# A two-layer streaming encoder: values of the memory as split products, keys 256 columns wide, and low parts of 35 chunks kept in DRAM

## Chip, cores and metric

The kernel runs on one core of one Trainium2 chip. The metric is the device time of one execution in microseconds; three executions of the kernel before took 1884.56, 1885.33 and 1886.70 us, a median of 1885.33. The execution that the profiler recorded took 1886.81 us.

## What is computed

One inference step of a small encoder of two layers, for 384 tokens of width 1024: 256 frames of a new stream (the prompt) and 8 running streams of 16 frames (the sample). Each layer is an FFN, a token mixer (a convolution module in layer 0, a gated DeltaNet in layer 1), cross-attention into 256 memory tokens, and a second FFN, each with a norm ahead of it and behind it.

```python
def trunk(x, mem_k, mem_v, conv_bufs, dn_states, dn_bufs, P):
    for i in range(DEPTH):
        x = x + 0.5 * post(swiglu(pre(x)))              # f00, f10
        x = x + post(conv(pre(x)) or deltanet(pre(x)))  # conv, dn
        x = x + post(memory_cross_attention(pre(x), mem_k[i], mem_v[i]))   # x0, x1
        x = x + 0.5 * post(swiglu(pre(x)))              # f01, f11

def conformer_conv_module(h, conv_buf, ...):
    val, gate = jnp.split(h @ w_in + b_in, 2, axis=-1)
    u = val * jax.nn.sigmoid(gate)
    c = causal_depthwise_conv(concat([conv_buf, u]), dw) + dw_b     # 31 taps
    return jax.nn.silu(layer_norm(c)) @ w_out + b_out

p_mem_k = jnp.einsum('bmd,lde->lbme', mem_prompt, xa_wk)
p_mem_v = jnp.einsum('bmd,lde->lbme', mem_prompt, xa_wv)
```

(The loop over the layers is shortened here; `post` and `pre` are RMS norms with gains.) The last two lines are what the change touches most: the keys and values of the memory, for both layers, are 256 x 1024 times 1024 x 1024 each. They don't depend on the tokens, are outputs of the kernel, and are read by the cross-attention of their layer. Everything is float32.

## The kernel before

**Two kinds of matmul.** Most products are made from split operands. A weight chunk (128 x 1024 numbers, 512 KB) is loaded into one of three `raw` buffers; ScalarE casts it to a rounded high part `whi` (type float32r) and VectorE subtracts, which gives the low part `wlo` (`Emitter.get`, with `act` at L189 and `tt` at L197). Both parts lie in one of eight slots (W = 8), which are handed out in turn; `done` gives a slot back. Activations are split in the same way (`hTh` and `hTl`, `rbh` and `rbl`). A product is then three matmuls: high x high, high x low, low x high. The other kind multiplies float32 as it is: each such matmul appears in the profile as two MATMUL records. The keys and values of the memory are of this kind.

**Memory jobs.** There are 32 of them (`kvq`): for each layer and each of four heads two for keys and two for values, each one chunk of 128 output columns. A job (`kv`) takes 16 matmuls of 128 columns, ScalarE copies the 128 x 256 result out, and a store on GpSimd's queue brings it to the output `out_pkv`. The memory itself (two chunks) and four chunk slots lie in a region of their own (`kv_open`). The table `KV` says how many jobs are put at which stage as filling: 3 at the start, 3 at the end of the first FFN, 20 in the convolution, 3 behind it, and 1 and 2 in the two FFNs that follow.

**Stages.** `ffn` goes through 22 slices f of the hidden width: a gate chunk and an up chunk (24 matmuls of 384 columns each), then a down chunk of an earlier slice (18 matmuls of 512 columns). The first FFN, f00, runs from about 24 to 297 us; from f = 10 on it also spawns `old_taps`, which computes those taps of the convolution that need only the cache. `conv` makes 8 pairs of gate and value chunks (`cg`, `cv`), each pair closed by `glu`; `taps` then goes through the 31 taps of two channel groups at a time on VectorE (`stt`, L210). After the last tap come the layer norm by token tiles (`ln`) and the output projection with 8 `co` chunks and the bias row `bout` (`tokenwise`), which prepares the next norm (`chain`).

**Order.** The program is written down as operations with costs, and `Scheduler.order` puts them in order for each engine by a list schedule: among the operations that are ready, the one goes first whose remaining path plus `bonus` is longest. The order on each engine is then fixed; an instruction that waits holds up those behind it on its engine. Loads (`load`, L283) are issued by SyncE's queue, stores (`store`, L286) by GpSimd's, which also computes the powers of the norms (L197, L204).

Of the kernel before, what the change touches and what calls it, by code (L numbers as in the profile page):

```python
# [8 lines left out]
F32 = mybir.dt.float32  # L9
F32R = mybir.dt.float32r  # L10
AF = mybir.ActivationFunctionType
ALU = mybir.AluOpType
# [3 lines left out]
P = 128  # L16
D = 1024
KT = 8
# [6 lines left out]
XH = 4  # L25
MEM = 256
# [6 lines left out]
START = ["c0a", "m0a", "c0b", "m0b", "m1", "i", "x1", "g", "c1", "x2", "x0", "c2"]  # L33
TOLD = CW - BL
OLD = 10
CHB = 4000.0
RUSH = 10000.0
NRUSH = 3
SLOTS = 4
FOUR = ["f01", "f10", "f11", "x0", "x1"]  # L40

SPLIT = {"f00": 0, "conv": 0, "x0": 1, "f01": 0, "f10": 0, "dn": 1, "x1": 2, "f11": 0}

KV = {"start": 3, "f00": 3, "conv": 20, "co": 3, "xo": 0, "f01": 1, "f10": 2, "dn": 6, "f11": 0}
HALF = 1400.0
# [22 lines left out]
def chunk_names():  # L68
    names = [("mem", 0), ("mem", 1), ("bout",)]
    for l in range(2):  # L70
        for i in range(2):
            for f in range(FF):
                names += [("g", l, i, f), ("u", l, i, f), ("d", l, i, f)]
            names += [(n, l, i, j) for n in ("g4", "u4") for j in range(4)]
        names += [("q4", l, 0, j) for j in range(4)]
        for k in range(KT):
            names += [("wq", l, k), ("wo", l, k), ("wk", l, k // 2, k % 2), ("wv", l, k // 2, k % 2)]
    for k in range(KT):
        names += [("cg", k), ("cv", k), ("co", k)]
    names.append(("ab",))  # L80
    for h in range(NH):
        names += [("q", h), ("k", h), ("v", h), ("z", h), ("do", h)]
    return names


CHUNK = {n: i for i, n in enumerate(chunk_names())}


# [5 lines left out]
class Emitter:  # L94
# [3 lines left out]
    def __init__(self, nc):  # L98
        self.nc = nc
        self.q = []  # L100
        self.vt = 0.0
        self.ck = {"A": 0.0, "V": 0.0, "G": 0.0}
        self.tasks = []
        self.nchunk = 0
        self.names = []
        self.dest = {}
        self.bonus = 0.0
# [181 lines left out]
    def get(self, name, dest=None):  # L289
# [9 lines left out]
        self.act(hi, raw)  # L299
        self.tt(lo, raw, hi.bitcast(F32), ALU.subtract)  # L300
        return j, hi, lo

    def done(self, j):
# [13 lines left out]
class Scheduler:  # L317
# [10 lines left out]
    def cell(self, ap):  # L328
# [6 lines left out]
        if r is not None:  # L335
            return r
        if name.startswith(("in_", "out_")):
            r = (name, ap.offset // (P * D)) if name == "out_pkv" else (None, 0)
# [155 lines left out]
class Model:  # L494
    def __init__(self, nc, tc, A, O, s, ps):
        self.nc, self.A, self.O = nc, A, O
        E = self.E = Emitter(nc)
        E.wall = A["w"]
        E.held = [None] * W
        E.tc = tc  # L500
# [20 lines left out]
        self.hready = [0.0] * TT  # L521
        self.kvq = [(k, l, h, i) for l in range(2) for h in range(XH) for k in ("wk", "wv") for i in range(2)]
        self.kvroom, self.kvs, self.kvn = None, {}, 0
# [230 lines left out]
    def ffn(self, l, i, chains, post, pre):  # L754
# [68 lines left out]
        for f in range(first, FF):  # L823
# [10 lines left out]
            up(f, *p, bg, ou, bu, eu)  # L834
            E.bonus = 0.0
            for _ in range(2):
                if ndown < min(f, FF - TAIL):
                    down(ndown)
                    ndown += 1
# [38 lines left out]
    def kv_open(self, slots=2, order=()):  # L878
# [13 lines left out]
        return True  # L892

    def early(self, what, order):

        self.E.bonus = 1e9 - 1e6 * order.index(what) if what in order else 0.0
# [19 lines left out]
    def kv(self, n):  # L916
# [11 lines left out]
        for _ in range(n):  # L928
# [6 lines left out]
            o, b = self.bank()  # L935
            for m in range(2):
                c = slice(m * P, (m + 1) * P)
                for k in range(KT):
                    a, b_ = (w[:, k, :], mem[:, k, c]) if kind == "wk" else (mem[:, k, c], w[:, k, :])
                    E.mm(o[:, c], a, b_, k == 0, k == KT - 1)  # L940
            E.act(res, o[:, 0:MEM], dep=0)
            self.bfree(b)
            dst = self.O["pkv"][l, h]
            if kind == "wk":
                E.store(dst[:, i * MEM:(i + 1) * MEM], res)
            else:
                E.store(dst[:, 512:1024].rearrange("p (m d) -> p m d", m=2)[:, :, i * P:(i + 1) * P],
                        res.rearrange("p (m d) -> p m d", m=2))
            if len(self.kvq) >= self.kvslots:
# [28 lines left out]
    def conv(self, chains, post, pre):  # L978
# [62 lines left out]
        prefetch(1)  # L1041
        for c in range(KT):
            if c == 0:
                (og, bg, eg), (ov, bv, ev) = self.first_chunks([("cg", c), ("cv", c)], chains, SPLIT["conv"])
            else:
                og, bg, eg = self.proj(("cg", c))
                ov, bv, ev = self.proj(("cv", c))
            glu(c, og, bg, eg, ov, bv, ev)
            if c + 2 < KT:
                prefetch(c + 2)  # L1050

        self.kv(KV["conv"])
        E.wait(tapper)
# [655 lines left out]
def pack(inp):  # L1709
# [14 lines left out]
    for n, i in CHUNK.items():  # L1724
# [3 lines left out]
        elif t == "bout":  # L1728
            w[i, 0] = f("ca_b_out")[0]
        elif t in ("g4", "u4", "q4"):  # L1730

            a = wq[n[1]] if t == "q4" else (wg if t == "g4" else wu)[n[1], n[2]]
            w[i] = a[n[3] * 256:n[3] * 256 + 256, 0:512].reshape(2, P, 512).transpose(1, 0, 2).reshape(P, D)
# [4 lines left out]
        elif t == "wq":  # L1738
            w[i] = g_type(wq[n[1]], n[2] * P)
        elif t in ("wk", "wv"):  # L1740
            w[i] = g_type((wk if t == "wk" else wv)[n[1]], n[2] * MEM + n[3] * P)
        elif t == "wo":
# [77 lines left out]
```

## Time and profile before

| | |
|---|---|
| time, median of three | 1885.33 us |
| profiled execution | 1886.81 us |
| its span, first to last instruction | 1885.0 us |
| TensorE (PE), busy | 1860.1 us, 99% |
| VectorE (DVE) | 1011.6 us, 54% |
| ScalarE (ACT) | 753.8 us, 40% |
| GpSimd (POOL) | 170.2 us, 9% |
| read from HBM, written | 265.09 MB, 11.92 MB |
| granted clock of TensorE | 0.999 |

Matmuls are pipelined, so a matmul's own duration in the profile is longer than the time after which the next one starts; where the cost of many matmuls is meant, the distance between starts is the number to use. The chain that ended last is the profile's account of what set the end: it goes back from the last instruction to what released it. A row of a window gives the busy time of each engine in a stretch of the span, the clock, the share of time that the DMA engines were busy and the rate in GB/s. "Idle before" and "<-" name what an engine waited for. The time "to landing" of a load runs from its issue to its arrival.

### The profile page before, as it was taken

Reading aid. Unit: us, or ns where it says so; the run is one execution under the profiler, and the core shown is the slowest. Engines: PE = TensorE matmul, PEld = TensorE weight load, DVE = VectorE, ACT = ScalarE, POOL = GpSimd, SP = SyncE. Lnnn points to the kernel's source line nnn. Section 1 sums busy time; section 2 is a strip of 40 time slices with the busy share of each in tenths; the row PEclk is TensorE's granted clock in tenths of the full one; section 3 lists DMA queues with packets and bytes.
Section 4 is the critical chain, followed back from the end, with each engine's and each line's share of the span. In section 5 each row is a group of like instructions: output and inputs, shape, how many; then the busy total and the mean of one; then the engine's idle time right before and its main releaser. Section 6 shows DMA issues by size and latency. Waiting matters only on the chain.

```text
span 1885.0 us, 27534 instructions
## 1 busy us (share of the span) xinstructions
PE 1860.1 (99%) x10895; PEld 1682.0 (89%) x10895; DVE 1011.6 (54%) x1708; ACT 753.8 (40%) x1435; POOL 170.2 (9%) x391
## 2 busy tenths in 40 slices
PE   8999999999999999999999999999999999999998
PEld 8999999999877899999899999999998766899997
DVE  6564436999553633333633333688776734533333
ACT  4333334312643632333433233676564534432332
POOL 1000002111100100000100000323221101000000
PEclk9999999999999999999999999999999999999999
DMA  8543434556686534434434333323325682444331
GB/s 303 178 136 126 134 112 122 127 147 219 213 314 216 157 123 134 132 125 130 154 115 131 123 124 111 118 79 116 126 93 165 228 316 74 137 132 135 123 123 45
DMA packets 88466, 278.81 MB, mean 148 GB/s; under 512 B 18001, under 2 KB 20561, under 8 KB 88337
## 3 DMA queue, kind: packets, MB, share of 16 engines
q1 hardware_dynamic: 86080, 271.42, 44.8%
q0 software_dynamic: 2256, 5.64, 0.9%
q8 instruction: 85, 1.39, 0.3%
q14 instruction: 45, 0.36, 0.1%
HBM read 265.09 MB, written 11.92 MB: 147 GB/s over the span
## 4 chain that ended last, share of the span: by engine, by line
PE 94%; DVE 1%; DMA 1%; ACT 1%; POOL 1%; issue 1%; SPq 0%; DVEq 0%; POOLq 0%; ACTq 0%
PE ps L247 89%; PE ps L279 3%; PE ps L259 2%; POOL stat L197 1%; DVE big L210 1%; ACT big L190 1%; DMA big<-in_cv 0%; DMA x<-in_x 0%; DMA raw<-in_w 0%; PE ps L272 0%; DVE big L197 0%; ACT hTl L190 0%; ACT whi L189 0%; DMA big<-in_state 0%; DVE wlo L197 0%
## 5 line engine op out<-in xcount | busy, mean ns | idle before, releaser
L197 DVE TENSOR_TENSOR wlo<-raw,whi 128x1024 fp32r<-128x1024 f32 x361 | 438.6, 1222 | 581.4 <-ACT whi L189 555.7
L189 ACT CAST whi<-raw 128x1024 fp32r<-128x1024 f32 x361 | 374.5, 1051 | 652.5 <-PE ps L247 603.5
L247 PE MATMUL ps<-hTh,wlo 128*128 128x384 f32 x1680 | 495.4, 339 | 0.0
L247 PE MATMUL ps<-hTh,whi 128*128 128x384 f32 (+1 forms) x1680 | 494.5, 340 | 0.1
L247 PE MATMUL ps<-hTl,whi 128*128 128x384 f32 x1680 | 493.8, 340 | 0.0
L247 PEld LDWEIGHTS ps<-hTh,whi 128*128 128x128 f32 x1680 | 308.7, 188 | 8.0 <-ACT big L190 1.0
L247 PEld LDWEIGHTS ps<-hTl,whi 128*128 128x128 f32 x1680 | 308.8, 188 | 6.9 <-issue 1.5
L247 PEld LDWEIGHTS ps<-hTh,wlo 128*128 128x128 f32 x1680 | 309.0, 188 | 4.2 <-issue 0.4
L247 PE MATMUL ps<-big 128*128 128x128 f32 (+3 forms) x1912 | 283.7, 286 | 9.9 <-DMA big<-in_w 6.4
L247 PEld LDWEIGHTS ps<-big 128*128 128x128 f32 x1912 | 256.7, 193 | 35.0 <-issue 17.8
L247 PE MATMUL ps<-whi,rbh 128*128 128x512 f32 x672 | 205.2, 396 | 0.4 <-DVE big L210 0.4
L247 PE MATMUL ps<-wlo,rbh 128*128 128x512 f32 x672 | 203.0, 395 | 0.0
L247 PE MATMUL ps<-whi,rbl 128*128 128x512 f32 x672 | 201.7, 394 | 0.0
L210 DVE SCALAR_TENSOR_TENSOR big<-big,cols 128x384 f32<-128x384 f32 (+13 forms) x424 | 189.3, 499 | 2.6 <-ACT big L190 0.3
L247 PEld LDWEIGHTS ps<-whi,rbl 128*128 128x128 f32 x672 | 125.7, 188 | 24.8 <-issue 0.4
L247 PEld LDWEIGHTS ps<-wlo,rbh 128*128 128x128 f32 x672 | 125.3, 188 | 24.6 <-issue 0.8
L247 PEld LDWEIGHTS ps<-whi,rbh 128*128 128x128 f32 x672 | 124.9, 188 | 20.5 <-DVE big L210 0.6
L279 PE MATMUL ps<-ident,big 128*128 128x128 f32 x479 | 86.0, 275 | 6.0 <-DVE big L210 5.6
L247 PE MATMUL ps<-whi,hTh 128*128 128x512 f32 x240 | 87.7, 401 | 0.2 <-ACT hTh L189 0.2
L197 DVE TENSOR_TENSOR big<-big,ps 128x384 f32<-128x384 f32 (+4 forms) x131 | 67.2, 519 | 36.2 <-PE ps L247 36.1
L247 PE MATMUL ps<-whi,hTl 128*128 128x512 f32 x240 | 86.4, 398 | 0.1
L204 POOL TENSOR_SCALAR stat<-stat 128x1 f32<-128x1 f32 (+2 forms) x48 | 16.8, 350 | 767.6 <-ACT hTl L190 754.0
(84 smaller groups left out, 1337.8 us busy)
## 6 DMA issues: line engine op xcount, KB each, us to landing
raw<-in_w SPq DMA_DIRECT2D x362, 512.0 KB, 3.7
big<-in_w SPq DMA_DIRECT2D x37, 512.0 KB, 4.7
big<-in_ck SPq DMA_DIRECT2D x32, 512.0 KB, 6.3
big<-in_cv SPq DMA_DIRECT2D x32, 512.0 KB, 6.6
big<-in_npre SPq DMA_DIRECT2D x8, 512.0 KB, 7.5
big<-in_npost SPq DMA_DIRECT2D x8, 512.0 KB, 6.2
out_pkv<-big POOLq DMA_DIRECT2D x32, 128.0 KB, 5.1
big<-out_pkv SPq DMA_DIRECT2D x8, 512.0 KB, 6.3
```

The costliest lines, as they stand in the source:

```text
L189: return self._on("A", cost, dep, lambda: sc.copy(out, in_), [in_], w)
L190: return self._on("A", cost, dep, lambda: sc.activation(out, in_, func, **kw), [in_, bias, scale] + ([] if after is None else [after]), w, ...
L197: return self._on(eng, cost, dep, lambda: e.tensor_tensor(out=out, in0=a, in1=b, op=op), [a, b], [out])
L204: return self._on(eng, cost, dep, lambda: e.tensor_scalar(out=out, in0=a, scalar1=s1, scalar2=s2, op0=op0, **kw), [a, s1, s2 if s2 is not ...
L210: lambda: v.scalar_tensor_tensor(out=out, in0=a, scalar=s, in1=b, op0=op0, op1=op1), [a, s, b], [out])
L247: self._add("P", cost, lambda: t.matmul(out, lhsT, rhs, start=start, stop=stop, **kw), [lhsT, rhs], [out])
L259: t.matmul(out, lhsT, rhs, start=start, stop=stop)
L279: self._add("P", 109.0, lambda: t.transpose(out, in_, ident), [in_, ident], [out])
```

## The change

- **Values.** The 16 value jobs leave `kvq`. A new function, `kv_split`, called in `conv` behind the eight input pairs, makes them as split products: the two memory chunks are split into `rbh` and `rbl`, and 16 new weight chunks `v4` (two k tiles x 512 columns each) go through `get`. Per layer and half there are 8 k tiles x 2 token tiles x 3 matmuls of 512 columns.
- **Keys.** A key job takes 8 matmuls of 256 columns in place of 16 of 128.
- **Low parts ahead.** For 35 chunks (`AHEAD`: the `cg` and `cv` chunks 4 to 7, the two memory chunks, 16 `v4`, `bout` and 8 `co`) the FFN f00 calls the new function `ahead`, two chunks per slice from f = 3 on: load, cast, subtract, and a store of the low part to a DRAM tensor `scr_lo`. Later, in the convolution, `get` of such a chunk loads and casts as usual, but its low part is loaded from DRAM, by a DMA on GpSimd's queue, in place of the subtraction.
- **Filling and order.** `KV` becomes 5 jobs in the convolution and 2 behind it (all key jobs now), `SLOTS` falls from 4 to 3, and the input pair c of the convolution has its priority lowered by 12000 x c.

```diff
+FIRST_AHEAD = 3
+ORD = 12000.0
-SLOTS = 4
+SLOTS = 3
-KV = {"start": 3, "f00": 3, "conv": 20, "co": 3, "xo": 0, "f01": 1, "f10": 2, "dn": 6, "f11": 0}
+KV = {"start": 3, "f00": 3, "conv": 5, "co": 2, "xo": 0, "f01": 1, "f10": 2, "dn": 0, "f11": 0}
+AHEAD = [(n, k) for k in range(4, KT) for n in ("cg", "cv")] + [("mem", 0), ("mem", 1)]
+AHEAD += [("v4", l, u, q) for l in range(2) for u in range(2) for q in range(4)] + [("bout",)] + [("co", k) for k in range(KT)]
...
         self.load(raw, self.wall[CHUNK[name]])
         self.act(hi, raw)
-        self.tt(lo, raw, hi.bitcast(F32), ALU.subtract)
+        if name in self.low:
+            self.store(lo, self.low.pop(name))
+        else:
+            self.tt(lo, raw, hi.bitcast(F32), ALU.subtract)
         return j, hi, lo
+
+    def ahead(self, name):
+        j, hi, lo = self.get(name)
+        self.low[name] = self.scr[self.nlow]
+        self.nlow += 1
+        self.store(self.low[name], lo)
+        self.done(j)
...
+            if (l, i) == (0, 0) and f >= FIRST_AHEAD:
+                for n in AHEAD[2 * (f - FIRST_AHEAD):2 * (f - FIRST_AHEAD) + 2]:
+                    E.ahead(n)
...
+    def kv_split(self):
+        mh, ml = (a.rearrange("p k c -> p (k c)")[:, 0:2 * D] for a in (self.rbh, self.rbl))
+        for i in range(2):
+            c = slice(i * D, (i + 1) * D)
+            E.get(("mem", i), dest=(mh[:, c], ml[:, c]))
...
+        for l in range(2):
+            for u in range(2):
+                (o, b) = self.bank2()
+                for q in range(4):
+                    j, wh, wl = E.get(("v4", l, u, q))
+                    for k in range(2 * q, 2 * q + 2):
+                        s = slice(512 * (k % 2), 512 * (k % 2) + 512)
+                        for m in range(2):
+                            c = slice(m * P, (m + 1) * P)
+                            E.mm(o[m], mh[:, k, c], wh[:, s], k == 0, False)
+                            E.mm(o[m], mh[:, k, c], wl[:, s], False, False)
+                            E.mm(o[m], ml[:, k, c], wh[:, s], False, k == KT - 1)
+                            E.pump()
+                    E.done(j)
+                for m in range(2):
+                    r = result(o[m], 512)
+                    for n in range(2):
+                        E.store(self.O["pkv"][l, 2 * u + n][:, 512 + m * MEM:512 + (m + 1) * MEM],
+                                r[:, n * MEM:(n + 1) * MEM])
+                self.bfree(b)
...
             o, b = self.bank()
-            for m in range(2):
-                c = slice(m * P, (m + 1) * P)
-                for k in range(KT):
-                    a, b_ = (w[:, k, :], mem[:, k, c]) if kind == "wk" else (mem[:, k, c], w[:, k, :])
-                    E.mm(o[:, c], a, b_, k == 0, k == KT - 1)
+            for k in range(KT):
+                E.mm(o[:, 0:MEM], w[:, k, :], mem[:, k, :], k == 0, k == KT - 1)
...
         for c in range(KT):
+            E.bonus = -ORD * c
...
             glu(c, og, bg, eg, ov, bv, ev)
+            E.bonus = 0.0
             if c + 2 < KT:
                 prefetch(c + 2)
+        self.kv_split()
         self.kv(KV["conv"])
```

More of the change, by code (lines that the diff above doesn't have):

```diff
@@ L76, in chunk_names @@
         for k in range(KT):
-            names += [("wq", l, k), ("wo", l, k), ("wk", l, k // 2, k % 2), ("wv", l, k // 2, k % 2)]
+            names += [("wq", l, k), ("wo", l, k), ("wk", l, k // 2, k % 2), ("v4", l, k // 4, k % 4)]
     for k in range(KT):
@@ L105, in __init__ @@
         self.names = []
-        self.dest = {}
+        self.low, self.nlow = {}, 0
         self.bonus = 0.0
@@ L336, in cell @@
             return r
-        if name.startswith(("in_", "out_")):
+        if name.startswith("scr_"):
+            r = ((name, ap.offset // (P * D)), 1)
+        elif name.startswith(("in_", "out_")):
             r = (name, ap.offset // (P * D)) if name == "out_pkv" else (None, 0)
@@ L498, in __init__ @@
         E.wall = A["w"]
+        E.scr = nc.dram_tensor("scr_lo", (len(AHEAD), P, D), F32R).ap()
         E.held = [None] * W
@@ L521, in __init__ @@
         self.hready = [0.0] * TT
-        self.kvq = [(k, l, h, i) for l in range(2) for h in range(XH) for k in ("wk", "wv") for i in range(2)]
+        self.kvq = [("wk", l, h, i) for l in range(2) for h in range(XH) for i in range(2)]
         self.kvroom, self.kvs, self.kvn = None, {}, 0
@@ L892, in kv_open, with result @@
         return True
+    def kv_split(self):
+        E = self.E
+        vt = E.vt
+        mh, ml = (a.rearrange("p k c -> p (k c)")[:, 0:2 * D] for a in (self.rbh, self.rbl))
+        for i in range(2):
+            c = slice(i * D, (i + 1) * D)
+            E.get(("mem", i), dest=(mh[:, c], ml[:, c]))
+        mh, ml = (a.rearrange("p (k m) -> p k m", k=KT) for a in (mh, ml))
+        res, rh = self.alloc(1024)
+        nres = [0]
+        def result(o, n):
+            r = res[:, nres[0] % 2 * 512:nres[0] % 2 * 512 + n]
+            nres[0] += 1
+            E.act(r, o[:, 0:n], dep=0)
+            return r
+        for l in range(2):
[18 more added lines that the diff above has]
+                self.bfree(b)
+        self.free(rh)
+        E.vt = vt
     def early(self, what, order):
@@ L935, in kv @@
             o, b = self.bank()
-            for m in range(2):
-                c = slice(m * P, (m + 1) * P)
-                for k in range(KT):
-                    a, b_ = (w[:, k, :], mem[:, k, c]) if kind == "wk" else (mem[:, k, c], w[:, k, :])
-                    E.mm(o[:, c], a, b_, k == 0, k == KT - 1)
+            for k in range(KT):
+                E.mm(o[:, 0:MEM], w[:, k, :], mem[:, k, :], k == 0, k == KT - 1)
             E.act(res, o[:, 0:MEM], dep=0)
             self.bfree(b)
[L943 to L948, printed above, removed]
+            E.store(self.O["pkv"][l, h][:, i * MEM:(i + 1) * MEM], res)
             if len(self.kvq) >= self.kvslots:
@@ L1729, in pack @@
             w[i, 0] = f("ca_b_out")[0]
-        elif t in ("g4", "u4", "q4"):
-            a = wq[n[1]] if t == "q4" else (wg if t == "g4" else wu)[n[1], n[2]]
+        elif t in ("g4", "u4", "q4", "v4"):
+            if t == "v4":
+                a = wv[n[1]][:, n[2] * 512:(n[2] + 1) * 512]
+            else:
+                a = wq[n[1]] if t == "q4" else (wg if t == "g4" else wu)[n[1], n[2]]
             w[i] = a[n[3] * 256:n[3] * 256 + 256, 0:512].reshape(2, P, 512).transpose(1, 0, 2).reshape(P, D)
@@ L1739, in pack @@
             w[i] = g_type(wq[n[1]], n[2] * P)
-        elif t in ("wk", "wv"):
-            w[i] = g_type((wk if t == "wk" else wv)[n[1]], n[2] * MEM + n[3] * P)
+        elif t == "wk":
+            w[i] = g_type(wk[n[1]], n[2] * MEM + n[3] * P)
         elif t == "wo":
```

## The prediction, made before the changed kernel was run

> **What bounds the kernel now.** I read the page first (busy shares, chain), then the chain in the convolution, then stage windows, then single rows.
>
> ```profile
> PE 1860.1 (99%) x10895; PEld 1682.0 (89%) x10895; DVE 1011.6 (54%) x1708; ACT 753.8 (40%) x1435; POOL 170.2 (9%) x391
> ...
> PE 94%; DVE 1%; DMA 1%; ACT 1%; POOL 1%; issue 1%; SPq 0%; DVEq 0%; POOLq 0%; ACTq 0%
> ```
>
> TensorE (PE) is 94% of the chain that sets the end, so PE time taken out is gained unless it comes back as idle PE. Two stages are touched: the first FFN (f00, about 24 to 297 us) and the convolution (about 297 to 503 us). The chain from 295 to 510 us, then windows (columns: stretch; length, PE; PEld; DVE; ACT; POOL; clock; DMA share; GB/s):
>
> ```profile
> 312.07 152.25 PE ps L247 x1116
> 465.13 1.20 issue
> 466.37 1.48 POOL stat L197
> 467.90 33.56 PE ps L247 x179
> ```
> ```profile
> 60.00:297.00 237.00, 237.00 (x1256) 222.06 (x1254) 112.08 (x176) 76.42 (x104) 2.27 (x7) 1.00 0.41 128
> 316.00:453.50 137.50, 137.50 (x1011) 136.18 (x1010) 127.46 (x272) 29.13 (x48) 25.20 (x41) 1.00 0.51 137
> 340.00:453.00 113.00, 113.00 (x869) 111.81 (x868) 110.19 (x236) 21.14 (x38) 20.57 (x33) 1.00 0.52 140
> 453.00:468.00 15.00, 14.57 (x111) 13.03 (x109) 11.23 (x14) 5.83 (x8) 4.28 (x6) 1.00 0.94 341
> 485.00:495.00 10.00, 10.00 (x46) 8.29 (x45) 3.55 (x5) 2.09 (x7) 2.30 (x5) 1.00 0.90 349
> ```
>
> F00 is PE alone: VectorE (DVE) is 47% busy, DMA 41%. From 340 to 453 us PE **and** DVE are both full (113.0 and 110.2 of 113 us): DVE with the taps, PE with memory jobs that fill the time the taps take. So the convolution shortens only by the smaller of what PE and DVE each save.
>
> **PE work.** Gaps between starts, from three timelines of PE:
>
> ```profile
> 409.83 15.35 PE L247 MATMUL ps<-big 128*128 128x128 f32 x136
> ```
> ```profile
> 570.18 1.02 PE L247 MATMUL ps<-big 128*128 128x256 f32 x4
> ```
> ```profile
> 28.30 0.33 PE L247 MATMUL ps<-hTh,wlo 128*128 128x384 f32 x1
> 28.48 0.33 PE L247 MATMUL ps<-hTh,whi 128*128 128x384 f32 x1
> ...
> 486.79 0.39 PE L247 MATMUL ps<-wlo,hTh 128*128 128x512 f32 x1
> 487.02 0.39 PE L247 MATMUL ps<-whi,hTh 128*128 128x512 f32 x1
> ```
>
> A full-precision matmul shows as two records. 128 columns: (15.35 - 0.28)/135 = 0.1116 us per record, the last record (0.28, the mean of its group) taken off. 256 columns: (1.02 - 0.38)/3 = 0.213 us. Split products: 0.173 us at 384 columns (28.48 to 28.65 repeats it, rounded 0.17), 0.227 at 512.
> - Removed: 32 memory jobs of 16 matmuls, 1024 records x 0.1116 = 114.3 us.
> - Keys back, 256 wide: 16 x 8 x 2 = 256 records x 0.213 = 54.5 us, against 57.1 for their half before. The widening alone is worth 2.6 us; if interleaving ate that, 0.
> - Values back, split: 2 layers x 2 halves x 8 x 2 x 3 = 192 matmuls x 0.227 = 43.6 us, against 57.1 before.
> - PE saves 114.3 - 98.1 = **16.2 us** (13.6 without the widening).
>
> **Where DVE lets it go.** In the convolution the change takes the subtraction that makes a low part off 17 of its chunks (8 input chunks, the bias row, 8 output chunks); the 18 chunks of values and memory get none there either. What stands there now, DVE first, then ScalarE (ACT):
>
> ```profile
> L197 DVE TENSOR_TENSOR wlo<-raw,whi x8: 1216/1220/1226, 322.0 to 363.8; 128x1024 fp32r<-128x1024 f32 x8
> ...
> 447.50 6.43 DVE L210 SCALAR_TENSOR_TENSOR big<-big,cols 128x384 f32<-128x384 f32 x12
> 453.85 1.22 DVE L197 TENSOR_TENSOR rbl<-raw,rbh 128x1024 fp32r<-128x1024 f32 x1
> 454.99 1.22 DVE L197 TENSOR_TENSOR wlo<-raw,whi 128x1024 fp32r<-128x1024 f32 x1
> ```
> ```profile
> 464.97 1.05 ACT L189 CAST whi<-raw 128x1024 fp32r<-128x1024 f32 x1 [2.09 <-DMA raw<-in_w]
> 467.79 1.04 ACT L189 CAST whi<-raw 128x1024 fp32r<-128x1024 f32 x1 [1.77 <-DMA raw<-in_w]
> 468.85 1.28 ACT L190 ACT_TABLE_LOAD   x1
> 470.14 3.57 ACT L190 ACTIVATE big<-big,cols 128x128 f32<-128x128 f32 x9
> 473.62 1.03 ACT L189 CAST hTh<-big 128x1024 fp32r<-128x1024 f32 x1
> ```
>
> The taps end at 453.85 us. The eight subtractions between 322 and 364 us are those of the eight input chunks that come ready-made now: start to start 1.14 us, so 9.1 us off, taps end near 444.7. From there to the end of the first cast for the output projection (473.62 + 1.03 = 474.65) are 20.8 us. Two casts in it wait for chunks (2.09 and 1.77 us) whose buffers were held by subtractions behind the taps; without these the casts come early. That frees up to 3 us: 18 to 20.8 us remain. The output projection starts 9 to 12 us sooner by DVE and ACT, where PE would allow 16.2. I take 12, because the subtractions at 453.85 and 454.99 leave as well. PE idles the missing **4 us** (bounds: 0, where the idle DVE of the stage closes up too, and 7). What is late next is then the taps themselves.
>
> Waits and queues: a ready-made low part is loaded by GpSimd's queue (POOL), which waits there until a slot of eight is free. Behind it stand the cache stores and, after the taps, the power of the norm, for which ACT waits. POOL has 20.6 busy us of 113, so I put the wait at nothing; uncovered, one late load costs its own landing, about 5 us.
>
> ```profile
> L286 POOL DMA_DIRECT2D out_pkv<-big x23 | 14.7, 640 | 66.0 <-ACT big L189 65.7 <-issue 0.3
> ```
>
> These 23 issues fell between 310 and 465 us, with DVE full of taps, at 640 ns each. The Trainium skill (SBUF — State Buffer, Who interferes with whom) says that some DVE forms shut GpSimd out of a shared port, and its part on the bandwidth-pool intuition has a DMA going from about 620 to 3100 ns that way; by that rule 35 loads would bring an estimated 87 us of POOL time, still under the stage. The row shows none of it for taps.
>
> **What f00 pays.** There, 35 chunks are loaded, cast, subtracted and stored, two per step of the loop. By page and windows:
>
> ```profile
> L197 DVE TENSOR_TENSOR wlo<-raw,whi 128x1024 fp32r<-128x1024 f32 x56 | 68.1, 1224 | 103.5 <-ACT whi L189 102.6
> L189 ACT CAST whi<-raw 128x1024 fp32r<-128x1024 f32 x55 | 56.6, 1049 | 127.7 <-PE ps L247 122.9 <-DMA raw<-in_w 4.5 <-ACT big L190 0.4
> ...
> big<-in_w SPq DMA_DIRECT2D x37, 512.0 KB, 4.7
> big<-in_ck SPq DMA_DIRECT2D x32, 512.0 KB, 6.3
> ...
> out_sstate<-big SPq DMA_DIRECT2D x8, 512.0 KB, 2.6
> ```
>
> DVE gains 35 x 1.22 = 43 us (112 + 43 of 237), ACT 35 x 1.05 = 37 us (76 + 37): both fit. DMA gains 35 reads and 35 writes of 0.524 MB, 36.7 MB in about 220 us: 128 + 167 = 295 GB/s, below the 349 seen. A store alone is 2.6 us by the nearest row. One slot fewer for key chunks costs nothing: a load lands in 4.7 us and the two other slots hold 6.8 us of PE work; without that cover it is 1.3 us a job. The tight part is the ring of three raw buffers. Casts of one burst, where the ring fills the slots as fast as it can, and landing times of its loads:
>
> ```profile
> 48.87 1.05 ACT L189 CAST whi<-raw 128x1024 fp32r<-128x1024 f32 x1 [2.59 <-DMA raw<-in_w]
> ...
> 65.19 1.05 ACT L189 CAST whi<-raw 128x1024 fp32r<-128x1024 f32 x1 [1.54 <-DMA raw<-in_w]
> ...
> DMA to landing us min/median/max: 4.2/4.5/4.8
> ```
>
> Eight casts, 16.32 us over seven gaps: **2.33 us a chunk**, three buffers in 7.0 us, of which 4.5 is landing and 2.5 the rest (cast, subtraction, hand-over). Needed: a step is 48 x 0.173 + 18 x 0.227 = 12.4 us of PE and now takes 5 chunks instead of 3, so 2.48 us each. Two stores a step hold the DMA engines some 1.3 us each by share (0.524 MB at about 400 GB/s, from 349 at a share of 0.90), a fifth of the time; landing may become 4.5 to 5.0, the ring 2.33 to 2.50. I take 2.48 to 2.50 and **1 us** lost at the start (bounds 0 and the rival below). Eight slots give about 5 chunks x 4.1 = 20 us of lead that must be used up before PE stands.
>
> **Sum**, against the profiled execution (1886.8 us, span 1885.0): -16.2 + 4 + 1 = -11.2, 1875.6. That execution lies 1.5 us above the median of the runs shown, so I predict 1885.3 - 11.2 = **1874.1 us**.
>
> **Rivals.**
> - *All of it arrives*: DVE's stage closes up by as much as PE saves and the ring holds. For it: 10 us of DVE are idle between 316 and 453.5 us before the taps end (127.46 of 137.5), so tap order has slack. Against: most of that is before the first taps. 1885.3 - 16.2 = 1869; with a shorter tail behind the taps 1867.
> - *The conv is short of data*: a value chunk brings 1.05 MB (raw and low) for 12 x 0.227 = 2.72 us of PE, 385 GB/s; the trace's full windows reach 341 to 349. At 345, 16 chunks take 48.7 us instead of 43.6; with their first landings, 5 to 7 us more: about 1880. Against: key jobs (0.52 MB for 3.4 us) and input projections can stand between. The Trainium skill (DMA: Bandwidth & Descriptors, Specifications) puts the share of HBM per core at about 358 GB/s; by it the estimate is 46.9 us for these chunks.
> - *The ring becomes f00's bound, and the kernel is slower*: with stores in the way landing goes to the 6.3 us of the cache loads. Then the ring gives (6.3 + 2.5)/3 = 2.93 us a chunk, 90 chunks 0.45 us late each, 40 us; less 20 of lead, 20 us of idle PE in f00: about 1893. It costs more than the change gains from 2.84 us a chunk, a landing of 6.0. For it: raw loads had up to 9.1 us in the loaded convolution. Against: median 5.0 there and 4.5 in the burst.
>
> ```profile
> DMA to landing us min/median/max: 3.5/5.0/9.1
> ```
>
> - *It doesn't do what it says*: casts through DRAM or the wider keys gain nothing, and idle takes the rest: 1885. The Trainium skill (DMA: Bandwidth & Descriptors, SWDGE vs HWDGE vs iDMA) says that a copy to float32r always casts; no row here has one, and it gives no rate.
>
> **How the numbers follow.** Forecast (1871 to 1879) 0.45; all of it 0.16; short of data 0.16; ring 0.15; nothing 0.08. 0.2% is 3.8 us, about what a measurement of this kernel tells from no change. Faster by over that: the first three, 0.77; within: 0.07; slower: ring and the rest, 0.16. Low end 1866, the best case with a microsecond beyond; high end 1888, which leaves out most of the ring and cuts through its milder forms. The forecast's own range is 1871 to 1879.
>
> **What will show it.** 256 key records at 0.213 us and 192 value matmuls at 0.227; the last tap at 443 to 446 us if f00 ends as now; the first cast for the output projection 9 to 13 us sooner, with a few us of idle PE ahead of it; in f00, PE without gaps and 2.4 to 2.5 us between casts. I am wrong if PE waits for weights in f00 ("DMA raw<-in_w" ahead of casts in tens of us), if POOL's loads of low parts are what PE's releases lead to, or if the taps end no sooner.

## The result, and the profile after

The changed kernel takes 1900.84 us (median of 4 executions, 1898.43 to 1901.49), the kernel before 1885.2 us on the same chip: a ratio of 1.0077, 95% interval 1.0064 to 1.0089. It is slower by 15.6 us where 11.2 less were forecast. The profiled execution took 1901.21 us, its span 1899.4 us.

From the page of the changed kernel: busy times, the chain that set the end, and the loads and stores with their time to landing.

```profile
PE 1856.5 (98%) x10319; PEld 1653.6 (87%) x10319; DVE 1034.0 (54%) x1726; ACT 808.1 (43%) x1480; POOL 200.2 (11%) x461
...
PE 79%; DMA 9%; issue 4%; ACT 4%; DVE 3%; POOL 1%; SPq 0%; POOLq 0%; ACTq 0%; DVEq 0%
...
scr_lo<-wlo POOLq DMA_DIRECT2D x35, 512.0 KB, 6.7
wlo<-scr_lo POOLq DMA_DIRECT2D x32, 512.0 KB, 8.3
```

PE had 94% of the chain before and has 79% now; DMA went from 1% to 9%. The busy totals hardly differ, so they don't say where. Marks do: the first update of the residual stream behind each stage, on DVE (the first of the two start times in a row). First the kernel before, behind f00 and behind the convolution; then the same of the changed kernel.

```profile
L210 DVE SCALAR_TENSOR_TENSOR x<-big,stat,x x6: 743/746/753, 291.7 to 306.0; 128x512 f32<-128x512 f32 x6
L210 DVE SCALAR_TENSOR_TENSOR x<-big,stat,x x6: 743/746/751, 494.8 to 517.2; 128x512 f32<-128x512 f32 x6
```
```profile
L215 DVE SCALAR_TENSOR_TENSOR x<-big,stat,x x6: 744/746/747, 306.6 to 318.0; 128x512 f32<-128x512 f32 x6
L215 DVE SCALAR_TENSOR_TENSOR x<-big,stat,x x6: 742/746/751, 508.4 to 530.5; 128x512 f32<-128x512 f32 x6
```

The mark behind f00 comes 14.9 us later (the last of the six updates 12.0 later, 318.0 after 306.0). From there to the mark behind the convolution it is 201.8 us after 203.1: 1.3 us gained where the prediction had 9 to 12. Counted from the last update behind f00 it is 190.4 us after 188.8, so the gain is missing by either count. Behind that 0.8 us more are lost, which makes up the 14.4 us between the two spans. So there are two things to explain: a loss in f00 and a gain that is missing in the convolution.

**F00.** Windows of the changed kernel (columns as in the prediction), over most of f00 and over two parts of the convolution; then the load ring in f00 (casts; landing time of its loads); then the largest waits of ACT and PE there (in total, times, longest).

```profile
60.00:300.00 240.00, 233.46 (x1215) 215.83 (x1214) 146.19 (x201) 109.93 (x127) 17.77 (x35) 0.99 0.81 269
...
410.00:456.00 46.00, 42.95 (x184) 34.00 (x183) 43.82 (x95) 17.98 (x23) 17.22 (x30) 1.00 1.07 324
...
440.00:500.00 60.00, 57.12 (x276) 47.24 (x275) 28.25 (x45) 31.82 (x52) 16.05 (x29) 1.00 1.04 364
```
```profile
L194 ACT CAST whi<-raw x89: 1039/1054/1061, 61.8 to 298.9; 128x1024 fp32r<-128x1024 f32 x89
...
DMA to landing us min/median/max: 3.4/5.0/8.4
```
```profile
ACT whi L194 <- DMA raw<-in_w: 124.9, 81, 3.8
...
PE ps L252 <- ACT big L195: 7.0, 9, 1.9
```

The DMA engines are busy 0.81 of the time (0.41 before), casts come every (298.9 - 61.8)/88 = 2.69 us, and most of them wait for their load (81 waits between 24 and 300 us). PE's waits are not for weights: they are for `big` of ACT, the SiLU of a slice (L195). One of the nine, in the timelines of ACT and of PE:

```profile
249.57 1.04 ACT L194 CAST whi<-raw 128x1024 fp32r<-128x1024 f32 x1 [1.57 <-DMA raw<-in_w]
250.52 0.48 ACT L195 ACTIVATE big<-ps 128x384 f32<-128x384 f32 x1
```
```profile
248.52 0.63 PE L252 MATMUL ps<-whi,rbh 128*128 128x512 f32 x2
251.05 0.45 PE L252 MATMUL ps<-hTh,whi 128*128 128x384 f32 x1 [1.90 <-ACT big L195]
```

ACT executes in the written order. The cast stands ahead of the SiLU and waits 1.57 us for its load; the SiLU starts only at 250.52, and PE has nothing to do until it has ended. The weights that lie ready in the slots don't help.

**Convolution.** First the chain of waits from 415 us on, then DVE around the last tap, then the first cast for the output projection:

```profile
414.98 1.06 ACT whi L194
416.06 9.25 DMA raw<-in_w
425.39 1.06 ACT whi L194
426.47 9.49 DMA raw<-in_w
436.06 1.06 ACT whi L194
437.13 10.01 DMA raw<-in_w
```
```profile
449.05 10.43 DVE L215 SCALAR_TENSOR_TENSOR big<-big,cols 128x384 f32<-128x384 f32 x16 [1.83 <-ACT big L194]
...
473.53 3.48 DVE L202 TENSOR_TENSOR big<-big,ps 128x1024 f32<-128x1024 f32 x3 [14.04 <-PE ps L252]
```
```profile
487.10 1.03 ACT L194 CAST hTh<-big 128x1024 fp32r<-128x1024 f32 x1
```

Before, PE alone was on the chain here (312 to 464 us). In this stretch the loads of value chunks are now: each takes 9 to 10 us, so three buffers give a chunk every 3.5 us where its matmuls take 2.72. The taps end at 449.05 + 10.43 = 459.5 us, 152.9 behind the f00 mark; before it was 453.85 (the first instruction behind them), 162.2 behind its own. That is the forecast 9.1 us (counted from the last update behind f00 it is 6.3). But then DVE waits 14.04 us for PE: the mean of the layer norm is a matmul, and its last part, at about 473 us, stands in PE's order behind the late value matmuls and behind 22 records of keys. From last tap to first cast it is 27.6 us instead of the 19.8 from 453.85 to 473.62.

PE falls short in an earlier stretch too, from 380 to 400 us, and there the DMA engines are not full. Its window, then the largest wait of PE between 316 and 500 us, then the chain at this place:

```profile
380.00:400.00 20.00, 15.55 (x71) 13.56 (x70) 20.00 (x46) 3.11 (x4) 2.52 (x4) 0.91 0.62 194
```
```profile
PE ps L252 <- DMA wlo<-scr_lo: 4.4, 2, 2.9
```
```profile
378.61 14.11 issue
392.74 5.73 DMA wlo<-scr_lo
398.51 10.75 PE ps L252 x52
```

Here PE waits for the low parts themselves: twice, 4.4 of the 10.8 us that it waits for others between 316 and 500 us. Their loads go through GpSimd's queue, through which the chain runs from 324 to 393 us, and the queue stands until PE gives back a slot (14.13 us before the load at 392.74); the landing comes on top of that. So the read-back costs in two ways: low parts that come late, and raw loads that come late.

### The profile page after: what moved, and what is told of

Its sections match the earlier page's. It is cut to its first block, busy times and chain, and to the rows that moved or that the text cites. A ratio compares the mean times of both kernels' runs of the same rounds, so it can differ in the third digit from the quotient of the medians.

```text
span 1899.4 us, 26710 instructions
## 1 busy us (share of the span) xinstructions
PE 1856.5 (98%) x10319; PEld 1653.6 (87%) x10319; DVE 1034.0 (54%) x1726; ACT 808.1 (43%) x1480; POOL 200.2 (11%) x461
## 4 chain that ended last, share of the span: by engine, by line
PE 79%; DMA 9%; issue 4%; ACT 4%; DVE 3%; POOL 1%; SPq 0%; POOLq 0%; ACTq 0%; DVEq 0%
PE ps L252 73%; DMA raw<-in_w 8%; PE ps L284 3%; PE ps L264 2%; ACT whi L194 2%; DVE wlo L202 2%; ACT big L195 1%; DVE big L215 1%; POOL stat L202 1%; DMA x<-in_x 0%; DVE big L202 0%; PE ps L277 0%; DMA big<-in_cconv 0%; POOL wlo L291 0%; ACT hTl L195 0%
## 5 line engine op out<-in xcount | busy, mean ns | idle before, releaser
L202 DVE TENSOR_TENSOR wlo<-raw,whi 128x1024 fp32r<-128x1024 f32 x380 | 462.4, 1223 | 572.3 <-ACT whi L194 544.6
L194 ACT CAST whi<-raw 128x1024 fp32r<-128x1024 f32 x412 | 429.8, 1053 | 698.5 <-PE ps L252 506.2
L252 PE MATMUL ps<-hTh,whi 128*128 128x384 f32 x1680 | 499.3, 340 | 7.2 <-ACT big L195 7.0
L252 PE MATMUL ps<-whi,rbh 128*128 128x512 f32 x736 | 232.2, 398 | 2.2 <-ACT whi L194 1.7
L252 PE MATMUL ps<-wlo,rbh 128*128 128x512 f32 x736 | 229.1, 397 | 4.5 <-DMA wlo<-scr_lo 4.4
L252 PE MATMUL ps<-big 128*128 128x128 f32 (+3 forms) x1144 | 214.9, 316 | 11.5 <-DMA big<-in_w 6.2
L252 PE MATMUL ps<-whi,rbl 128*128 128x512 f32 x736 | 226.1, 395 | 0.0
L252 PEld LDWEIGHTS ps<-big 128*128 128x128 f32 x1144 | 176.4, 192 | 40.4 <-issue 14.6
L215 DVE SCALAR_TENSOR_TENSOR big<-big,cols 128x384 f32<-128x384 f32 (+11 forms) x424 | 191.4, 504 | 4.7 <-ACT big L194 1.8
L252 PEld LDWEIGHTS ps<-wlo,rbh 128*128 128x128 f32 x736 | 138.4, 189 | 33.2 <-DMA wlo<-scr_lo 5.5
```

The costliest lines, as they stand in the source:

```text
L194: return self._on("A", cost, dep, lambda: sc.copy(out, in_), [in_], w)
L202: return self._on(eng, cost, dep, lambda: e.tensor_tensor(out=out, in0=a, in1=b, op=op), [a, b], [out])
L215: lambda: v.scalar_tensor_tensor(out=out, in0=a, scalar=s, in1=b, op0=op0, op1=op1), [a, s, b], [out])
L252: self._add("P", cost, lambda: t.matmul(out, lhsT, rhs, start=start, stop=stop, **kw), [lhsT, rhs], [out])
```

## The experiments

What costs time is tested for each loss by itself. In f00: the stores of low parts (DMA time), the loads, the depth of the ring, or the order on ACT. In the convolution: the bytes of low parts read back, the depth of the ring, or the taps. Marks are the first updates behind f00 and behind the convolution, as above; the same code gave them within 2 us of each other in different kernels (f00 306.6 and 306.0 in the changed kernel and e3, 295.3 and 297.1 in e2 and e6). Each kernel is planned anew by the list schedule, which counts the bytes of every transfer, so an edit can also change the order on the engines; for e2, e3 and e12 their traces were compared for it.

**E1: four raw buffers.**

```diff
-RAW = 3
+RAW = 4
-BIG = 17300
+BIG = 16276
```

> The changed kernel with four raw buffers in place of three (the general region gives up 1024 columns). The changed kernel took 1900.8 us, its first FFN f00 made its first residual update at 306.6 us where it was 291.7 before, and its casts there came every 2.66 us. Theory (ring): f00 is paced by the three raw buffers, each held for landing (5.0 us) plus 3.0 us, so four of them give 2.0 us a chunk, under the 2.48 that are needed: first update at 292 to 295 us, no casts waiting in tens of us, total 1880 to 1888 us. Rival (bytes): 283 GB/s with stores in between is what the DMA engines give, a fourth buffer only makes landing longer: first update still at 303 us or later, total 1897 to 1902 us.

1912.34 us, 1.0148 [1.0131, 1.0165]. The windows at the start and over f00:

```profile
20.00:60.00 40.00, 37.60 (x193) 35.35 (x192) 33.41 (x65) 19.52 (x26) 2.41 (x5) 0.91 0.81 270
60.00:300.00 240.00, 239.35 (x1262) 223.80 (x1262) 149.35 (x210) 108.75 (x131) 18.21 (x35) 1.00 0.82 277
```

Between 60 and 300 us PE is full again, with 47 records more than in the changed kernel: a deeper ring does cover the late loads there. But the f00 mark stays at 307.1 us, as the rival had it: the start lost 24 records against the changed kernel (217 there in the same window) and clock (0.91). The larger ring leaves 1024 columns less of common buffer, which may be the reason; that was not tested. Some of the f00 delay is left unaccounted for by this. In the convolution the fourth buffer gains 1.0 us (200.8 from mark to mark): loads in flight land later, a median of 8.8 us after 8.3. The 11.5 us to the changed kernel were lost behind the convolution; the common buffer also serves the later stages, and what there costs how much was not separated.

**E2: no stores in f00; e3: low parts read back at 64 of 1024 columns; e6: both.**

```diff
# e2_nostore
-            self.store(lo, self.low.pop(name))
+            self.low.pop(name)
+            self.store(lo, self.wall[CHUNK[name]])
...
-        self.store(self.low[name], lo)
# e3_lo64
-            self.store(lo, self.low.pop(name))
+            self.store(lo[:, 0:64], self.low.pop(name)[:, 0:64])
```

> The changed kernel without the 35 stores of low parts in f00 (work left out: the low parts later come from the weight chunks themselves, 35 reads of the same size in the convolution). Theory (ring): landing falls from 5.0 to about 4.5 us, the ring to (4.5 + 3.0)/3 = 2.5 us a chunk, just what is needed: first update of f00 at 293 to 298 us, total 1887 to 1892 us. Rival (the stores themselves, by the bytes or by the slots that they hold): the whole loss of f00 goes, first update at 291 to 293 us. If neither ring nor stores matter (VectorE and ScalarE with 35 chunks more): first update still at 303 us or later.

> The changed kernel with the low parts read back in the convolution cut to 64 of their 1024 columns (work left out: the rest of each low part holds old data), 1.1 MB in place of 18.4 MB. From f00's first update to the first update behind the convolution are 201.8 us in the changed kernel, 203.1 before, 191 by the prediction. Theory (bytes in the convolution): with 17 MB less the loads land in 5 us and the distance falls to 190 to 194 us, total 1889 to 1893 us. Rival (order and slots, POOL waits for PE to free a slot and PE waits for that low part): the distance stays at 199 to 203 us, total 1898 to 1902 us. f00 stays as it is, first update at 305 to 308 us, by both.

> The changed kernel with both costs of the way through DRAM taken out: no stores in f00, and the low parts read back in the convolution cut to 64 of 1024 columns (work left out; the rest of a low part holds old data). Without the stores alone it took 1887.6 us, with the narrow reads alone 1892.3, the changed kernel 1900.8. Theory (two separate costs, 13.2 and 8.5 us): they add, 1877 to 1881 us, under before (1885.8). Rival (one cost that moves from the one stage to the other): 1884 to 1888 us.

Without the stores 1887.62 us, 1.0010 [1.0001, 1.0020]; with the short read-back 1892.31, 1.0032 [1.0019, 1.0045]; with both 1878.51, 0.9954 [0.9939, 0.9969]. Of the 15 us above the kernel before, the stores are 13.2, and the read-back is 8.5; the sum, 21.7, is what both together take off (22.3). E2: window, landing and ACT's wait in f00, then both marks.

```profile
60.00:300.00 240.00, 240.00 (x1263) 224.40 (x1262) 152.83 (x211) 116.19 (x143) 3.20 (x11) 1.00 0.65 204
...
DMA to landing us min/median/max: 3.4/4.3/5.3
...
ACT whi L194 <- DMA raw<-in_w: 79.4, 53, 5.1
...
L215 DVE SCALAR_TENSOR_TENSOR x<-big,stat,x x6: 739/740/746, 295.3 to 306.7; 128x512 f32<-128x512 f32 x6
L215 DVE SCALAR_TENSOR_TENSOR x<-big,stat,x x6: 742/744/751, 495.9 to 518.0; 128x512 f32<-128x512 f32 x6
```

The loads, casts and subtractions of the 35 chunks are all still there, and PE is full; the f00 mark moves 11.3 us to the front. The 48 records more, at 240/1263 = 0.19 us, are 9.1 us of it. Two other readings fall away by the traces: in the changed kernel no engine waits for a store to land in f00, so it is not that the stores keep slots occupied; and on ACT as many casts stand ahead of each SiLU in e2 as in the changed kernel, or one more, so it is not a better order there. The convolution still takes 200.6 us. E3, the chain from 395 to 470 us, the window in which the changed kernel's PE waited for low parts, and the two marks:

```profile
by line: PE ps L252 89.7%; DMA raw<-in_w 5.8%; ACT whi L194 4.2%; ACT big L194 0.4%; issue 0.2%
...
380.00:400.00 20.00, 20.00 (x104) 18.43 (x103) 20.00 (x46) 5.03 (x7) 3.08 (x5) 1.00 0.44 112
...
L215 DVE SCALAR_TENSOR_TENSOR x<-big,stat,x x6: 742/745/747, 306.0 to 319.0; 128x512 f32<-128x512 f32 x6
L215 DVE SCALAR_TENSOR_TENSOR x<-big,stat,x x6: 744/746/751, 497.5 to 520.2; 128x512 f32<-128x512 f32 x6
```

With a sixteenth of the low parts' bytes and the same number of low-part loads on GpSimd's queue the convolution takes 191.5 us, PE has the chain again and waits for no low part, and raw loads land after 4.5 us (median) instead of 8.3. So the missing gain is the price of the read-back, and not of the taps, of PE's work or of issuing these loads. It is not shown that the bytes alone make this price: planned with fewer bytes, PE and GpSimd have some instructions of the convolution in another order, from 324 us on GpSimd and from 379 us on PE. E12, below, keeps PE's order and halves the bytes in DRAM; it gets 4.6 us.

**E4: 26 chunks ahead, spread evenly; e5: casts planned later; e9: both.** Left to VectorE as before: the low parts of `bout` and `co`. The second edit raises the landing time that the list schedule assumes for every DMA, which puts casts further behind in ACT's order.

```diff
# e4_ahead26
-AHEAD += [... for q in range(4)] + [("bout",)] + [("co", k) for k in range(KT)]
+AHEAD += [... for q in range(4)]
-                for n in AHEAD[2 * (f - FIRST_AHEAD):2 * (f - FIRST_AHEAD) + 2]:
+                for n in AHEAD[(f - FIRST_AHEAD) * 26 // 19:(f - FIRST_AHEAD + 1) * 26 // 19]:
# e5_order: this alone; e9_ahead26_order: both
-DMA_IN, DMA_OUT = 650.0, 950.0
+DMA_IN, DMA_OUT = 650.0, 2300.0
```

> The changed kernel with 26 chunks ahead in place of 35 (the bias row and the 8 output chunks make their low part in the convolution as before), spread evenly over the 19 slices from f = 3 on: 4.37 chunks per slice of 12.4 us, so 2.84 us each are at hand where the ring takes 2.66. Theory (ring): f00 no longer loses, first update at 292 to 296 us; the subtractions come behind the taps, where VectorE is 28% busy, and 4.7 MB less are read there: total 1882 to 1889 us. Rival (each chunk ahead costs f00 a share, whatever the pace): 26/35 of 14.9 us remain, first update at 302 to 304 us, total 1896 us or more.

> The changed kernel with one constant of the planner altered: it takes a load to land 2300 ns after its transfer in place of 950, so that it plans with 4.9 us from issue to landing (5.0 measured in f00 of the changed kernel, 3.7 of before). Buffers and work are the same, only the order on the engines differs, in all stages. Theory (the queue of ScalarE): PE stands in f00 because a SiLU stands behind a cast that waits for its raw load; planned with later landings the casts come behind the SiLU. Waits of PE and of its weight loads for ScalarE in f00 (7.0 and 11.2 us) go under 3 us, the last residual update of f00 comes at 306 to 311 us (318.0; 306.0 before), total 1886 to 1895 us. Rival (the ring's rate alone): the chunks come no faster, PE then waits for weights instead: last update at 316 us or later, total 1898 us or more.

> 26 chunks ahead, evenly spread, planned with the later landing (2300 ns). With 26 ahead and the old plan f00's last update came at 314.5 us (before 306.0, 35 ahead 318.0), although 2.84 us a chunk are at hand, more than the ring's 2.66. Theory (two things: the ring's rate at 35 chunks; at 26 chunks the order on ScalarE, where a SiLU stands behind a cast that waits): with the rate no longer binding the other order now helps, last update at 306 to 310 us. Rival (f00 pays for every chunk ahead, whatever rate and order): 313 to 316 us. Total by the first about 1905 us or less, since the convolution of this spread lost too (1917.3 with the old plan); by the second 1914 us or more.

E4: 1917.34 us, 1.0168 [1.0151, 1.0185]. E5: 1909.48, 1.0122 [1.0109, 1.0136]. E9: 1909.98, 1.0123 [1.0106, 1.0140]. All are slower than the changed kernel, but what each does to f00 tells ring and order apart. At f00 the rivals were right in e4 and e5, the theory in e9. The f00 marks of e4 and e9, then PE's waits in f00 of e5:

```profile
L215 DVE SCALAR_TENSOR_TENSOR x<-big,stat,x x6: 742/746/751, 302.8 to 314.5; 128x512 f32<-128x512 f32 x6
```
```profile
L215 DVE SCALAR_TENSOR_TENSOR x<-big,stat,x x6: 742/744/750, 294.9 to 306.9; 128x512 f32<-128x512 f32 x6
```
```profile
PE ps L252 <- ACT whi L194: 4.6, 4, 1.3
PE ps L252 <- DVE wlo L202: 3.7, 8, 0.7
```

At 35 chunks the later plan takes the wait from the SiLU and gives it to the weights (8.3 us in place of 7.0), and the mark stays at 306.6: the ring itself is short. At 26 chunks the old plan still loses (302.8), the later plan nothing against e2 (294.9, PE full): there it was only the order on ACT. Both e4 and e9 then lose more in the convolution (221.2 and 216.8 us from mark to mark), where VectorE makes nine low parts again; PE waits up to 9.6 us for VectorE in one place (e9). That the nine are the cause was not tested by itself, and e9's total fits neither of the two that were named. The later plan also costs some 8 us behind the convolution, in stages that this change doesn't touch (the two marks of e5 and of the changed kernel agree within 0.2 us, and their times are 8.6 us apart).

**E7: nothing ahead.** `AHEAD = []`: VectorE makes every low part in the convolution.

> The changed kernel with no chunk ahead: split values and wide keys as in the change, but all low parts by VectorE in the convolution. Theory (the convolution is bound by VectorE): f00 as before (last update 306 us), 18 subtractions more between the taps than before, 1.14 us each, so the last tap near 474 us in place of 453 and a total of 1900 to 1908 us; PE's 16 us are lost in waiting. Rival (PE's work decides, subtractions find gaps): last tap under 460 us and 1872 to 1885 us.

1919.36 us, 1.0176 [1.0162, 1.0190]. F00 marks at 293.6, the convolution takes 233.4 us. VectorE near the end of the taps:

```profile
489.45 1.22 DVE L201 TENSOR_TENSOR wlo<-raw,whi 128x1024 fp32r<-128x1024 f32 x1
490.59 1.26 DVE L214 SCALAR_TENSOR_TENSOR big<-big,cols 128x384 f32<-128x384 f32 x2
491.77 1.22 DVE L201 TENSOR_TENSOR wlo<-raw,whi 128x1024 fp32r<-128x1024 f32 x1
```

The subtractions stand between the taps, which end at 491.8 us. That is 18 us later than the theory had it; why so much was not traced. In this kernel split values pay only with ready-made low parts, and only if these come cheaply (e6 against e7). Its f00 mark also says what the 35 chunks cost without their stores: 295.3 - 293.6 = 1.7 us.

**E8: the keys alone**, on the kernel before.

```diff
-            for m in range(2):
+            if kind == "wk":
+                for k in range(KT):
+                    E.mm(o[:, 0:MEM], w[:, k, :], mem[:, k, :], k == 0, k == KT - 1)
+            for m in range(2 if kind == "wv" else 0):
...
```

> The kernel before with one part of the change: keys as 8 matmuls of 256 columns in place of 16 of 128; values, filling and low parts as before. By the rows 0.213 us per record of 256 columns against 2 x 0.1116: 16 jobs save 2.6 us of PE. Theory (PE sets the end): 1882 to 1884.5 us. Rival (the filling only makes room for VectorE's taps, at least 10 of the 16 jobs lie in that stage): 1884.5 to 1886 us, no change that can be told.

1885.62 us, 0.9998 [0.9990, 1.0007]: no change. Its window over the taps:

```profile
340.00:453.00 113.00, 113.00 (x722) 107.93 (x721) 110.71 (x237) 21.12 (x38) 20.97 (x33) 1.00 0.51 141
```

VectorE is as full as before (110.71 of 113 us). PE time saved without taking any from VectorE is filled with other work, as the prediction had it: the smaller of the two savings counts.

**E10 and e11: half of it.** Only the values of layer 0 are split, 18 chunks go ahead, one per slice from f = 4; the values of layer 1 stay as they were (13 jobs in the convolution). Then the same with the later plan.

```diff
-AHEAD += [("v4", l, u, q) for l in range(2) ...] + [("bout",)] + [("co", k) ...]
+AHEAD += [("v4", 0, u, q) for u in range(2) for q in range(4)]
...
# e11_half_order also:
-DMA_IN, DMA_OUT = 650.0, 950.0
+DMA_IN, DMA_OUT = 650.0, 2300.0
```

> Half the change: values of layer 0 alone as split products, those of layer 1 as 8 memory jobs as before, wide keys, 18 chunks ahead (8 input chunks, the memory, 8 value chunks), one per slice from f = 4 on; 13 jobs in the convolution. PE saves 6.7 us by the values and up to 2.6 by the keys, VectorE loses 9 us among the taps, 9.4 MB go through DRAM in place of 18.4. Theory (both costs come from the amount that goes through DRAM): f00's last update at 306 to 310 us, the convolution 6 to 9 us shorter than before, total 1877 to 1883 us. Rival (late chunks cost in proportion): half of the losses of 13.2 and 8.5 us, 1886 to 1891 us.

> The same half change, planned with the later landing (2300 ns). With 35 chunks the later plan cost 8.6 us in all (1909.5 against 1900.8), about as much in stages behind the convolution as before them. Theory (order matters in f00 as long as the ring's rate does not bind): f00's last update at 306 to 308 us, but 3 to 6 us lost behind the convolution, total 1882 to 1888 us. Rival (order makes no difference in f00): last update as in the half change with the old plan, and the total 3 to 8 us above it.

1922.71 us, 1.0193 [1.0177, 1.0208], and 1917.08, 1.0162 [1.0147, 1.0177]. Both are far slower than their theories had them, and e10 than its rival too. Even at one chunk a slice the old plan puts the f00 mark at 301.9; with the later plan it is 293.5. In e10 PE waits for others only 1.6 us between 24 and 300 us; there the chain at the end of f00 goes through a cast that waits 6.64 us for its load, ahead of the norm's work on ACT. The convolution takes 224.2 and 220.7 us, longer than before the change. Between 316 and 500 us PE waits 12.2 us for chunks of memory jobs and 10.8 for low parts in e10, and 14.0 us for VectorE in e11, which has the low parts of `bout` and `co` back. Which of the edits does this was not separated. In this form a smaller dose is no way out.

**E12: low parts in bfloat16 in DRAM**, half the bytes.

```diff
-        E.scr = nc.dram_tensor("scr_lo", (len(AHEAD), P, D), F32R).ap()
+        E.scr = nc.dram_tensor("scr_lo", (len(AHEAD), P, D), mybir.dt.bfloat16).ap()
```

> The changed kernel with the low parts kept in DRAM in two bytes per number in place of four: the same 70 transfers, half of their bytes on the DRAM side. Theory (bytes): landing in f00 falls from 5.0 towards 4.6 us, f00's last update to 310 to 313 us, the distance over the convolution from 201.8 to 195 to 198 us, total 1886 to 1892 us. Rival (a transfer costs by its number, or by the 4 KB per row on the SBUF side): nothing changes, 1899 to 1903 us.

1897.00 us, 1.0055 [1.0040, 1.0070]: 3.8 us better than the changed kernel, still slower than before. Its windows over f00 and the convolution, and the landing of raw loads in f00:

```profile
60.00:300.00 240.00, 232.26 (x1217) 214.93 (x1216) 148.19 (x203) 110.72 (x128) 18.32 (x36) 1.00 0.81 234
400.00:440.00 40.00, 37.09 (x163) 29.92 (x163) 40.00 (x91) 16.05 (x21) 13.56 (x23) 1.00 1.04 307
...
DMA to landing us min/median/max: 3.4/5.1/8.9
```

The rate falls from 269 to 234 GB/s, but the DMA engines are busy 0.81 as before and the raw loads land no sooner; the f00 mark gains 1.6 us, no more than such marks differ by. The convolution gains 4.6 (197.2), with PE's records in the same order as in the changed kernel. The total lies between theory and rival. In f00 the landing thus goes with the time that the DMA engines are busy, and half the bytes in DRAM did not make that time shorter.

## Why the prediction was wrong

- *PE sets the end, and its work falls by 16.2 us*: the terms held. In the changed kernel the 16 records of a key job take 3.61 us, (3.61 - 0.38)/15 = 0.215 each (0.213 predicted); nine value matmuls start between 451.44 and 453.25 us, 0.226 us apart (0.227 predicted).

```profile
453.48 3.61 PE L252 MATMUL ps<-big 128*128 128x256 f32 x16
```

- *The widened keys are worth 2.6 us*: not alone (e8, 0). The bound of 0 named there was right, since the taps set the stretch.
- *Taps end 9.1 us sooner, the output projection 9 to 12*: the taps, yes (9.3 from mark to mark). The output projection was 1.4 us sooner, 180.5 instead of 181.9 us behind the f00 mark. With the read-back cut short it was 10.2 (e3) and 11.0 (e6), from casts at 477.71 and 468.00 us. So this reading of VectorE was right, and what failed is the sentence that put the loads of low parts *at nothing, or at 5 us for a late one*. PE waited 4.4 us for late low parts, near that 5; the step that was missing is that these loads also delay the raw loads, and those the values. The rival "short of data" had the second at 5 to 7 us. The read-back cost 8.5 by time and 10.3 by the marks (e3): the raw loads' median landing rose from 5.0 to 8.3 us, where the rival counted only bytes at a full rate, and the late low parts are in it too.
- *F00 pays 1 us*: the failed step that costs most. Without stores it pays 1.7 us (e2 against e7), with them 13.0. The landing was foreseen, 4.5 to 5.0 us (median 5.0), but it went into a ring of average times, 2.48 to 2.50 us a chunk. The loads spread from 3.4 to 8.4 us, and the casts came every 2.69 us where e2, with PE full, had 91 casts from 61.0 to 296.3, one each 2.61: 88 x 0.08 = 7 us short over the stage. The *20 us of lead* in the slots did not have to be used up first. ACT executes its casts and its SiLUs in one order, so a late load stops PE with weights in the slots (7.0 us in nine waits).
- *The rival "ring becomes f00's bound"* had the right place and sign, with the wrong threshold: it was to decide from 2.84 us a chunk and a landing of 6.0. At 2.69 and 5.0 f00 lost 11.3 us to the stores. Its price of 20 us was lateness less 20 us of lead. The lead held for the weights (PE waits for none in f00), but it does not cover a SiLU behind a late cast.
- *POOL's queue and the slot fewer*: in the changed kernel PE waits for no chunk of a key job between 316 and 500 us, so the slot is no cost there. POOL's queue is on the chain: its wait for a free slot, put at nothing, comes ahead of both late low parts. What it would cost with loads that land soon is not known; e3 keeps the queue and has the gain, with another order on it. Issuing was cheap. The 32 loads took 553 ns to issue, amid taps:

```profile
L291 POOL DMA_DIRECT2D wlo<-scr_lo x32 | 17.6, 553 | 86.4 <-PE ps L252 82.8 <-DMA wlo<-scr_lo 2.4 <-DMA out_pconv<-big 0.8
```

The Trainium skill (SBUF — State Buffer, Who interferes with whom) would have some VectorE forms shut GpSimd out; its part on the bandwidth-pool intuition has a DMA from GpSimd go from about 620 to about 3100 ns beside one such form, a copy. The trace shows none of that for these taps. The Trainium skill's share of HBM per core, about 358 GB/s (DMA: Bandwidth & Descriptors, Specifications), is near the 364 GB/s of the window from 440 to 500 us; in the stretch that counts, 410 to 456 us, the DMA engines were full at 324.

- *The sum*: -11.2 was forecast for the whole. With both DMA costs taken away the chip gives 1878.51 against 1886.1, -7.6. The two costs, 22.3 us together, were forecast at 1; the 3.6 us between -11.2 and -7.6 are not assigned.
- *The signs of being wrong*: two of the three came. Casts in f00 waited 124.9 us for their loads, though PE then waited for SiLUs and not for weights; and two of PE's waits ended with a load of a low part. The third did not: behind the f00 mark the taps ended sooner.

What is open: by the first update 1.9 us of the f00 delay are there without anything ahead (e7), but by the last of the six e7 is not late (305.1 us, 306.0 before), so this is the spread of the updates and need not be a loss. How the price of the read-back splits between late low parts and late raw loads was not separated by a run, and whether another order of the low parts' loads in the convolution would hide them was not tried.

## What to carry to other kernels

Precomputing in an idle-looking stage and parking the result in DRAM cost DMA time twice here, and both times the loads that were already there landed later: price such a detour by how much later those land, and by the landing of what comes back, not by the free share of the DMA engines. Where one engine executes in order both load-bound work and work that the bottleneck waits for, ready weights are no cover; a late load passes straight on. Test each half of such a trade by itself: leaving out only the stores, or shrinking only the read-back, told in which stage the time went. And look at the order too: a planner that counts bytes answers such an edit with another order.

## What was not expected of the hardware

- The DMA engines' busy share did not follow the bytes: with low parts in bfloat16 f00 moved 234 instead of 269 GB/s at the same share of 0.81 and the same landing.
- With a fourth raw buffer the raw loads in the loaded convolution landed later (median 8.8 us after 8.3), and the stage gained only 1.0 us.
- Once, a lower clock followed a short stop of PE: in the 10 us that hold the wait of 1.90 us shown above, the longest of the nine in f00, the granted clock was 0.83, an estimated (1 - 0.83) x 10 = 1.7 us lost. In the 10 us around each of the other eight it was 1.00.

```profile
250.00:260.00 10.00, 8.95 (x37) 7.92 (x38) 4.77 (x6) 4.68 (x6) 0.61 (x2) 0.83 0.95 284
```
